# Making all modulation columns of a hybrid layer on TensorE: one change to the opening of a kernel

## The chip, the cores and the metric

The kernel runs on one core of a Trainium2 chip. A core has five engines that run side by side, each through its own list of instructions in order: TensorE (PE in the profile; it multiplies and transposes into the PSUM banks), VectorE (DVE), ScalarE (ACT), GpSimd (POOL) and SyncE (SP, which here issues the loads and stores). They wait for one another through semaphores. The metric is the device time of one execution in microseconds (us), the median over runs.

## The reference

One layer over 1024 latent tokens and 256 context tokens of width 1024, batch 1, in float32:

```python
sh1, sc1, g1, sh2, sc2, g2 = split(silu(c) @ w_ada + b_ada, 6)
csh1, csc1, *_             = split(silu(c_ctx) @ w_ada + b_ada, 6)
hx = rmsnorm(x, norm1_g) * (1 + sc1) + sh1
hc = rmsnorm(ctx, norm1_g) * (1 + csc1) + csh1
# hx @ w_in, hc @ w_in feed neighbourhood attention (with the context keys),
# two-way retention and two gates
x = x + g1 * merge(attention, retention)
x = x + g2 * conv_ffn(rmsnorm(x, norm2_g) * (1 + sc2) + sh2)
out = rmsnorm(x, final_norm_g)
```

The case is about the first two lines: shift and scale of the first modulation, for the latent tokens (from c) and for the context (from c_ctx). That is 2 x 1024 values for each of the two vectors, each a sum over 1024 products.

## The kernel before

**Layout.** Channels lie in the partitions after a transpose: a block kb of 128 channels (kb = 0 to 7) is a tile of 128 partitions by tokens. Tokens come in two halves of 512 (half 0 and 1) and one context block of 256. A shift or scale column is one number per partition for a block; `acol` holds them by vector s (0 for c, 1 for c_ctx), block kb and kind i (0 shift, 1 scale).

**The opening** (about the first 90 us of the profile) makes the modulated input and the first projection. Its pieces, with the lines under which the profile shows them:

- `load_x(tb)` loads a block of 128 tokens (8 latent ones, 8 and 9 are context). `square_x` (L162, ScalarE) sums squares, `rstd_x` (L166, L167, GpSimd) makes the inverse root, `scale_x` (L170, VectorE) scales the block in place.
- `transp(tb, (kb,), tag)` (L197, TensorE) transposes one 128 x 128 piece into a PSUM tile of its channel block. PSUM tiles come from three rings: "c0" and "c1" with three banks each, later the sums of the first projection, and "tp" with two banks, through which everything else goes. `evac_t` (L205) copies such a tile to SBUF (tile low) to free its bank.
- `mod_h` (L217, ScalarE) writes scale*x + shift rounded to the high part (tile hx, or hc for the context), `mod_v` (L221, VectorE) the same in full (tile vh or vc), `mod_l` (L226, VectorE) the difference, the low part. `ctx_h`, `ctx_v`, `ctx_l` are these three for a context block of channels.
- `load_first(half)` loads three weight blocks of the first projection (q, k and v of a head pair), `split_hi` (L319, ScalarE) and `split_lo` (L322, VectorE) split them into high and low parts. `first_mm(half, kb)` (L121 to L123, TensorE) does nine matmuls of 512 columns: three products of high and low parts for q, k and v. It needs both parts of the block's modulated input; for kb of 4 and more it needs the weights of load_first(1).
- `load_bc(i)` loads one of the vectors c and c_ctx broadcast over partitions (tile cs), `silu_bc(i)` (L245, ScalarE) takes its SiLU. `decays(h)` (L553 to L558) makes six exponentials of one column for a retention head; they are the first to need another function table, whose load the profile shows as ACT_TABLE_LOAD.
- `next_load`, `next_hi` (L589), `next_lo` (L592) bring the first weights of the second head pair; `next_mm` and `ctx_mm` (L110 to L112) are the projections behind the opening. In between, `ev_hi` and `ev_lo` (L401 to L419) move the sums of the first projection out of PSUM: q, k and v of the first head pair. next_mm writes into two banks that the ring "tp" has used.

**Two ways to a column.** The constant NPE = 2 divides the blocks.

- Blocks 0 to 3 come in two groups of two blocks, on TensorE: `load_ag(g, q)` loads a quarter of the group's weights (512 KB), `ag_mm(g, q)` (L259) multiplies SiLU of both vectors (two columns) with it, 512 wide, in two matmuls of float32, each two instructions in the profile. After four quarters `ag_ev` (L263) copies the resulting two rows to SBUF, `ag_tr` (L268) turns them into columns in four small transposes, `ag_fin` (L274, L275, VectorE) adds the bias and multiplies the scales with the norm's gain.
- Blocks 4 to 7 come as sums over a row: `load_ada(kb)` loads shift and scale weights of a block, transposed (two tiles of 512 KB). Each of the 16 sums is either one multiply-and-sum on VectorE (`ada_stt`, L297) or a product on GpSimd (`ada_prod`, L303) and a sum on ScalarE (`ada_sum`, L307); eight of each. `ada_fin` (L292, L293) adds bias and gain.

**Order.** The opening stands in `with tc.manual_schedule()`: each engine executes its pieces in the order of the text. What follows (attention by head pairs, retention by heads, the merge, the conv-FFN) is ordered by a planner, apart from a few groups. Rings of buffers set when loads can start: 14 tiles of 512 KB hold the token blocks and the modulation weights, three tiles of 256 KB the raw projection weights.

Of the kernel before, what the change touches and what calls it, by code (L numbers as in the profile page):

```python
# [11 lines left out]
ALU = mybir.AluOpType  # L12
# [21 lines left out]
NPE = 2  # L34
# [6 lines left out]
def tile_hybrid_layer(ctx, tc: tile.TileContext, io, dbg=None):  # L41
# [190 lines left out]
    cs2 = [(s0 if i else csp).tile([P, D], F32, name=f"cs{i}") for i in range(2)]  # L232
    wad = {}
# [7 lines left out]
    def load_bc(i):  # L241
        sync.dma_start(cs2[i], io["cvec"][i : i + 1].to_broadcast([P, D]))

    def silu_bc(i):
        act.activation(cs2[i], cs2[i], AF.Silu)  # L245
# [34 lines left out]
    def load_ada(kb):  # L280
        wad[kb] = [s_tile("x", 14) for _ in range(2)]
        for i in range(2):
            sync.dma_start(wad[kb][i], io["w_ada1"][kb - 2 * NPE, i])


    acol = cpool.tile([P, 2, KB, 2], F32, name="acol")

    def ada_fin(kb, s, eng):
        t = acol[:, s, kb]
        eng = pool if eng == "pool" else vec  # L290
        bb = cst["b"][:, 0:16].rearrange("p (i k) -> p i k", i=2)
        eng.tensor_tensor(t, t, bb[:, :, kb], ALU.add)  # L292
        eng.tensor_tensor(t[:, 1:2], t[:, 1:2], cst["g"][:, 0, kb : kb + 1], ALU.mult)  # L293
        (ca if s else cx)[kb] = (t[:, 1:2], t[:, 0:1])

    def ada_stt(kb, s, i):
        vec.scalar_tensor_tensor(s_tile("aj", 1), wad[kb][i], 1.0, cs2[s], ALU.mult, ALU.mult, accum_out=acol[:, s, kb, i : i + 1])  # L297

    prods = {}

    def ada_prod(kb, s, i):
        prods[kb, s, i] = s_tile("prod", 3)
        pool.tensor_tensor(prods[kb, s, i], wad[kb][i], cs2[s], ALU.mult)  # L303
# [232 lines left out]
    def ada_col2(i):  # L536
        w = ada2[i]
        late(vec.scalar_tensor_tensor(w, w, 1.0, cs2[0], ALU.mult, ALU.mult, accum_out=col[:, 16 + i : 17 + i]))  # L538
        if i + 1 < 32:
            ada_load()  # L540
# [71 lines left out]
    with tc.manual_schedule():  # L612
# [124 lines left out]
        load_bc(0)  # L737
        silu_bc(0)
        load_first(1)
        load_ada(4)  # L740
        ada_prod(4, 0, 1)
# [16 lines left out]
        load_ada(6)  # L758
# [8 lines left out]
        split_lo(1, 2)  # L767
        mod_v(True, 1, 2)
# [32 lines left out]
        ada_stt(5, 0, 0)
        square_x(9)
        ada_prod(6, 0, 0)
        ada_sum(6, 0, 0)
        mod_v(True, 1, 4)
        ada_prod(6, 0, 1)
        ada_sum(6, 0, 1)
        ada_stt(5, 0, 1)
        square_x(8)
        mod_l(True, 1, 4)  # L810
        ada_fin(6, 0, "pool")
        mod_v(True, 0, 6)
        mod_h(True, 1, 6)
        transp(4, (5,), ("tp",))
        transp(5, (5,), ("tp",))
        first_mm(0, 4)
# [3 lines left out]
        ada_fin(5, 0, "pool")  # L820
        mod_h(True, 1, 5)
        mod_v(True, 1, 6)
        mod_h(True, 0, 5)
        first_mm(1, 4)
        rstd_x(8, 2)
        scale_x(9)
        mod_h(True, 0, 6)
        silu_bc(1)
        scale_x(8)
        transp(8, (2,), ("tp",))  # L830
        transp(9, (2,), ("tp",))
        ctx_h(2)
        mod_l(True, 1, 6)
        first_mm(1, 6)
        transp(8, (0,), ("tp",))
        mod_v(True, 1, 5)
        mod_l(True, 1, 5)
        decays(1)
        ctx_v(2)
        ctx_l(2)  # L840
        mod_l(True, 0, 6)
        transp(8, (6,), ("tp",))
        transp(9, (0,), ("tp",))
        transp(9, (6,), ("tp",))
        ctx_h(0)
        evac_t(False, 0, 6, "act")
        next_load(0)
        load_ada(7)
        ada_prod(7, 0, 1)
        ada_sum(7, 0, 1)  # L850
        ada_stt(7, 0, 0)
        first_mm(0, 6)
        ctx_v(0)
        ada_prod(4, 1, 0)
        ada_sum(4, 1, 0)
        transp(8, (5,), ("tp",))
        mod_v(True, 0, 5)
        ctx_l(0)
        mod_l(True, 0, 5)
        ada_prod(7, 1, 0)  # L860
        transp(8, (1,), ("tp",))
        transp(9, (1,), ("tp",))
        ctx_v(1)
        ctx_h(1)
        transp(9, (5,), ("tp",))
        evac_t(False, 0, 5, "act")
        first_mm(1, 5)
        ada_stt(6, 1, 1)
        decays(3)
        transp(8, (3,), ("tp",))  # L870
        transp(9, (3,), ("tp",))
        transp(8, (4,), ("tp",))
        ctx_h(3)
        ada_prod(5, 1, 0)
        ada_fin(7, 0, "vec")
        ada_stt(7, 1, 1)
        ctx_v(3)
        mod_v(True, 1, 7)
        mod_v(True, 0, 7)
        ctx_l(1)  # L880
        mod_h(True, 0, 7)
        transp(9, (4,), ("tp",))
        mod_h(True, 1, 7)
        mod_l(True, 1, 7)
# [1186 lines left out]
```

## Time and profile before

| | before |
|---|---|
| median of 3 runs | 1781.46 us (1779.99 to 1782.4) |
| the profiled execution | 1783.34 us |
| its span, first to last instruction | 1781.6 us |
| mean granted TensorE clock | 0.988 |
| busy share of the span: PE, DVE, ACT, POOL | 97%, 73%, 48%, 32% |
| moved by DMA | 261.62 MB, mean 147 GB/s |

In a line of the timeline stand the start, the duration, the engine, the line of the code, the operation with its output and input tiles and their sizes, and how many instructions were merged; in brackets the idle time before and who ended it. Durations of matmuls overlap, so their cost is the distance from start to start. In the views of stretches, a line has the stretch, its length, busy time of the engines, the granted clock of TensorE (1.00 is full), the DMA share and GB/s. In the view of a tile stand the least, median and greatest duration in ns, and the first and last start. Windows of time are in us from the start of the span.

### The profile page before, as it was taken

The numbers are of one execution on the slowest core, as the hardware profiler recorded it, in microseconds if no ns is written. First come the engines' busy times: TensorE is split into PE (matmuls) and PEld (weight loads), VectorE is DVE, ScalarE is ACT, GpSimd is POOL, SyncE is SP. The second block draws the span as 40 slices with busy tenths as digits, with TensorE's granted clock in tenths as the row PEclk, the third lists the DMA queues.
The fourth block names the chain that finished last, engine by engine and source line by source line (L and its number), as shares of the span: only waits on it lengthen the run. The fifth ranks groups of instructions, "written<-read, shape, count | busy, mean of one in ns | idle before, by whom it ended". The sixth has DMA issues, their size and how long they took to land.

```text
span 1781.6 us, 24740 instructions
## 1 busy us (share of the span) xinstructions
PE 1728.4 (97%) x8357; PEld 1431.6 (80%) x8357; DVE 1309.0 (73%) x2458; ACT 850.2 (48%) x1833; POOL 569.1 (32%) x477
## 2 busy tenths in 40 slices
PE   8799999999999999999999999989999999999997
PEld 3588888888888888778877888868888888788886
DVE  5878888765776766777655556879989989875755
ACT  5667666652443434443444333544444444554444
POOL 2610000002334343554412400065555555211444
PEclk9899999999999999999999999999999999999999
DMA  9133334432231212677558633642332332586754
GB/s 344 57 116 119 113 111 137 140 112 101 70 107 48 72 39 71 205 234 252 177 178 277 224 140 138 238 137 89 107 101 89 108 118 101 165 285 195 241 160 160
DMA packets 139552, 261.62 MB, mean 147 GB/s; under 512 B 15872, under 2 KB 28320, under 8 KB 139424
## 3 DMA queue, kind: packets, MB, share of 16 engines
q1 hardware_dynamic: 139424, 260.03, 43.6%
q8 instruction: 66, 1.08, 0.3%
q14 instruction: 62, 0.51, 0.1%
HBM read 187.87 MB, written 69.48 MB: 144 GB/s over the span
## 4 chain that ended last, share of the span: by engine, by line
PE 41%; issue 6%; DVE 4%; POOL 3%; DMA 2%; ACT 1%; SPq 0%; POOLq 0%; ACTq 0%; DVEq 0%
PE u L1374 28%; PE y L1374 4%; PE pr L110 2%; PE pr L111 2%; PE pr L112 2%; PE om L121 1%; PE om L122 1%; PE om L123 1%; DVE wc L87 1%; POOL x L1885 1%; DMA ur<-in_w_up 0%; DVE v L1662 0%; DMA raw<-d_orr 0%; DVE b L1350 0%; POOL pd L1922 0%
## 5 line engine op out<-in xcount | busy, mean ns | idle before, releaser
L1374 PE MATMUL u<-T,wc 128*128 128x512 f32 x960 | 227.9, 393 | 6.4 <-ACT pu L1408 5.8
L1374 PEld LDWEIGHTS u<-T,wc 128*128 128x128 f32 x960 | 180.9, 189 | 47.6 <-ACT pu L1408 9.1
L1374 PE MATMUL y<-wc,ahl 128*128 128x512 f32 x924 | 210.7, 390 | 3.3 <-DVE wc L87 1.8
L1374 PEld LDWEIGHTS y<-wc,ahl 128*128 128x128 f32 x924 | 173.4, 188 | 40.3 <-DVE wc L87 2.5
L87 DVE TENSOR_TENSOR wc<-ur,wc 128x512 fp32r<-128x512 f32 x137 | 125.3, 917 | 65.2 <-ACT wc L86 65.1
L86 ACT CAST wc<-ur 128x512 fp32r<-128x512 f32 x137 | 85.1, 622 | 129.9 <-PE y L1374 72.1
L111 PE MATMUL mm<-low,wc 128*128 128x512 f32 (+1 forms) x328 | 124.1, 378 | 0.0
L1374 PE MATMUL u<-h2a,wc 128*128 128x512 f32 x480 | 112.3, 390 | 0.7 <-DVE pu L1417 0.7
L110 PE MATMUL mm<-hx,wc 128*128 128x512 f32 x264 | 107.5, 407 | 0.3 <-DVE vc L221 0.3
L1374 PEld LDWEIGHTS u<-h2a,wc 128*128 128x128 f32 x480 | 90.1, 188 | 19.8 <-DVE pu L1417 1.2
L112 PE MATMUL mm<-hx,wc 128*128 128x512 f32 x264 | 105.2, 399 | 0.0
L86 ACT CAST wc<-s 128x512 fp32r<-128x512 f32 x80 | 49.7, 622 | 91.5 <-PE u L1374 86.9
L123 PE MATMUL mm<-wc,low 128*128 128x512 f32 (+1 forms) x240 | 91.3, 380 | 0.0
L1508 POOL TENSOR_TENSOR col<-col,bcol 128x32 f32<-128x32 f32 x1 | 0.3, 253 | 281.5 <-DVE aw L538 281.5
L1374 PE MATMUL u<-hxT,wc 128*128 128x512 f32 x384 | 89.6, 389 | 0.0
L87 DVE TENSOR_TENSOR wc<-s,wc 128x512 fp32r<-128x512 f32 x80 | 86.4, 1082 | 2.4 <-ACT wc L86 2.0
L1374 PEld LDWEIGHTS u<-hxT,wc 128*128 128x128 f32 x384 | 72.1, 188 | 14.9
L87 DVE TENSOR_TENSOR wc<-raw,wc 128x512 fp32r<-128x512 f32 x92 | 69.5, 763 | 18.2 <-ACT wc L86 18.1
L1383 POOL TENSOR_TENSOR s<-ur 128x512 f32<-128x512 f32 x20 | 36.7, 1835 | 125.1 <-DVE wc L87 71.7
L121 PE MATMUL mm<-wc,hx 128*128 128x512 f32 x192 | 75.3, 392 | 0.6 <-ACT r L1105 0.6
L122 PE MATMUL mm<-wc,hx 128*128 128x512 f32 x192 | 75.3, 392 | 0.0
L86 ACT CAST wc<-raw 128x512 fp32r<-128x512 f32 x92 | 56.7, 621 | 32.0 <-DMA raw<-in_w_pret 5.3
(393 smaller groups left out, 4722.7 us busy)
## 6 DMA issues: line engine op xcount, KB each, us to landing
ur<-in_w_up SPq DMA_DIRECT2D x80, 256.0 KB, 3.0
ur<-d_a SPq DMA_DIRECT2D x77, 256.0 KB, 3.1
aw<-in_w_ada SPq DMA_DIRECT2D x32, 512.0 KB, 3.2
pj<-in_w_down SPq DMA_DIRECT2D x44, 256.0 KB, 4.8
d_w<-pj SPq DMA_DIRECT2D x44, 256.0 KB, 2.0
d_a<-sa SPq DMA_DIRECT2D x44, 256.0 KB, 2.0
ur<-d_w SPq DMA_DIRECT2D x44, 256.0 KB, 3.7
d_a<-at SPq DMA_DIRECT2D x33, 256.0 KB, 2.7
```

What stands on the lines that cost most here:

```text
L86: act.copy(hi, src)
L87: (lo_eng or vec).tensor_tensor(lo, src, hi.bitcast(F32), ALU.subtract)
L110: pe.matmul(out, wh, xh, start=k == 0, stop=False)
L111: pe.matmul(out, wh, xl, start=False, stop=False)
L112: pe.matmul(out, wl, xh, start=False, stop=k == n - 1)
L121: pe.matmul(out, ah, bh, start=first, stop=False)
L122: pe.matmul(out, ah, bl, start=False, stop=False)
L123: pe.matmul(out, al, bh, start=False, stop=last)
L1374: pe.matmul(out, a, b, start=first and n == 0, stop=last and n == 2, skip_group_check=True)
L1383: pool.tensor_tensor(self.s1, self.a21, self.a22, ALU.add)
L1508: pool.tensor_tensor(col[:, 16:48], col[:, 16:48], bcol[:, 16:48], ALU.add)
L1885: pool.tensor_tensor(z, z, fg[:, gs(dh)], ALU.mult)
```

## The change

NPE becomes 4, so all eight blocks go through load_ag, ag_mm, ag_ev, ag_tr and ag_fin in four groups. load_ada, ada_stt, ada_prod, ada_sum and ada_fin are gone, and so is one of the two broadcast vectors; the other is still loaded, later, since a later stage uses it. The weights of all groups are laid out on the host as those of groups 0 and 1 were.

```diff
-NPE = 2
+NPE = KB // 2
...
-    cs2 = [(s0 if i else csp).tile([P, D], F32, name=f"cs{i}") for i in range(2)]
-    wad = {}
+    cs2 = csp.tile([P, D], F32, name="cs")
...
-    def load_bc(i):
-        sync.dma_start(cs2[i], io["cvec"][i : i + 1].to_broadcast([P, D]))
+    def load_bc():
+        sync.dma_start(cs2, io["cvec"][0:1].to_broadcast([P, D]))
...
-    def load_ada(kb):
...
-    def ada_fin(kb, s, eng):
...
-    def ada_stt(kb, s, i):
-        vec.scalar_tensor_tensor(s_tile("aj", 1), wad[kb][i], 1.0, cs2[s], ALU.mult, ALU.mult, accum_out=acol[:, s, kb, i : i + 1])
...
-    def ada_prod(kb, s, i):
-        prods[kb, s, i] = s_tile("prod", 3)
-        pool.tensor_tensor(prods[kb, s, i], wad[kb][i], cs2[s], ALU.mult)
...
-    def ada_sum(kb, s, i):
-        t = prods[kb, s, i]
-        act.activation(t, t, AF.Copy, accum_out=acol[:, s, kb, i : i + 1])
...
-    w1 = w_ada[:, :2048].reshape(4, 2, P, 2, KB // 2, 2 * P)
-    out["w_ada1g"] = ac(w1[:, :, :, :, :NPE].transpose(4, 0, 2, 1, 3, 5).reshape(NPE, 4, P, 1024))
+    w1 = w_ada[:, :2048].reshape(4, 2, P, 2, NPE, 2 * P)
+    out["w_ada1g"] = ac(w1.transpose(4, 0, 2, 1, 3, 5).reshape(NPE, 4, P, 1024))
-    out["w_ada1"] = ac(w_ada[:, :2048].T.reshape(2, KB, P, D).transpose(1, 0, 2, 3)[2 * NPE :])
```

The order of the opening stays up to `first_mm(0, 3)`. From there the new text reads as follows, several calls to a line. T stands for the latent grid (True), and transp(4-7, 5) for the four calls of token blocks 4 to 7 with channel block 5; mod(half, kb) stands for mod_h, mod_v and mod_l of that block in this order, ctx(kb) for ctx_h, ctx_v and ctx_l.

```
load_first(1)  load_ag(2,0) load_ag(2,1)  transp(6,4) transp(6,7)  split_hi(1,2)  scale_x(7)
transp(7,4) transp(6,2) transp(6,0) transp(7,2) transp(7,0) transp(6,1) transp(7,1)
mod_v(T,1,1)  evac_t(T,1,4,act)  mod_h(T,1,0)  transp(7,7)  evac_t(T,1,7,act)
load_ag(2,2) load_ag(2,3)  mod_v(T,1,0) mod_l(T,1,0)  mod_h(T,1,1)  evac_t(T,1,2,act)  mod_h(T,1,2)
transp(4-6,6)  split_lo(1,2)  mod_l(T,1,1)  mod_v(T,1,2)
first_mm(0,2)  transp(4-7,3)  evac_t(T,1,3,act)  transp(7,6)  evac_t(T,1,6,act)
load_ag(3,0) load_ag(3,1)  split_hi(1,1)
first_mm(1,0)  mod_l(T,1,2)  ag_mm(2,0) ag_mm(2,1)  load_ag(3,2) load_ag(3,3)  mod_v(T,1,3) mod_h(T,1,3)
first_mm(1,1)  ag_mm(2,2) ag_mm(2,3)  ag_ev(2,act)  mod_l(T,1,3)  split_lo(1,1)  load_x(9) load_x(8)
first_mm(1,2)  ag_tr(2)  ag_fin(2)  split_hi(1,0)  mod(0,4)  split_lo(1,0)  transp(4-7,5)
first_mm(1,3)  mod(1,4)  load_bc()  load_ex()
first_mm(0,4)  ag_mm(3,0) ag_mm(3,1)  mod(0,5)  next_load(0)
first_mm(1,4)  ag_mm(3,2) ag_mm(3,3)  ag_ev(3,act)  mod(1,5)  square_x(9) square_x(8)  rstd_x(8,2)
first_mm(0,5)  ag_tr(3)  ag_fin(3)  mod(0,6)
first_mm(1,5)  mod(1,6)  scale_x(9) scale_x(8)
first_mm(0,6)  transp(8-9,2) transp(8-9,0)  mod(0,7)  ctx(2)
first_mm(1,6)  transp(8-9,1)  mod(1,7)  ctx(0)  next_hi(0)  transp(8-9,3)
first_mm(0,7)  ctx(1) ctx(3)  transp(8-9,4) transp(8-9,5)  ctx(4)  next_lo(0)  silu_bc()  decays(1)  ctx(5)
first_mm(1,7)  transp(8-9,6) transp(8-9,7)  decays(3)  ctx(6) ctx(7)  decays(0) decays(2)  dec_scale()  next_load(1)
```

Before, the same stretch went as follows (the modulations of halves and blocks in single steps, mixed with the sums):

```
first_mm(0,3)  load_bc(0) silu_bc(0)  load_first(1)  load_ada(4)  ada_prod(4,0,1) ... scale_x(7) ... load_ada(6) ...
first_mm(0,2) ... ada_sum(4,0,1) ... load_x(9)  load_bc(1)  load_ada(5)  ada_stt(4,0,0)
first_mm(1,0) first_mm(1,1)  ada_fin(4,0)  first_mm(1,2) ... load_ex()  load_x(8) ... ada_stt(5,0,0)  square_x(9)
ada_prod(6,0,0) ada_sum(6,0,0) ... ada_prod(6,0,1) ada_sum(6,0,1)  ada_stt(5,0,1)  square_x(8)  ada_fin(6,0) ...
first_mm(0,4) first_mm(1,3)  ada_fin(5,0) ... first_mm(1,4)  rstd_x(8,2)  scale_x(9)  silu_bc(1)  scale_x(8) ...
first_mm(1,6) ... decays(1) ... next_load(0)  load_ada(7)  ada_prod(7,0,1) ada_sum(7,0,1)  ada_stt(7,0,0)
first_mm(0,6) ... ada_prod(4,1,0) ada_sum(4,1,0) ... ada_prod(7,1,0) ...
first_mm(1,5)  ada_stt(6,1,1)  decays(3) ... ada_prod(5,1,0)  ada_fin(7,0)  ada_stt(7,1,1) ...
first_mm(0,5) first_mm(1,7)  ada_prod(6,1,0) ada_sum(7,1,0) ada_fin(7,1) ada_sum(5,1,0) ... ada_stt(4,1,1) ... next_hi(0) next_lo(0)
decays(0) ... ada_fin(4,1) ... ada_stt(5,1,1) ... ada_sum(6,1,0) ... decays(2)  ada_fin(5,1) ... ctx_l(6)  dec_scale()
first_mm(0,7)  next_load(1)
```

More of the change, by code (lines that the diff above doesn't have):

```diff
@@ L819, in tile_hybrid_layer @@
         first_mm(1, 3)
-        ada_fin(5, 0, "pool")
-        mod_h(True, 1, 5)
+        mod_h(True, 1, 4)
+        mod_v(True, 1, 4)
+        mod_l(True, 1, 4)
+        load_bc()
+        load_ex()
+        first_mm(0, 4)
+        ag_mm(3, 0)
+        ag_mm(3, 1)
+        mod_h(True, 0, 5)
+        mod_v(True, 0, 5)
+        mod_l(True, 0, 5)
+        next_load(0)
+        first_mm(1, 4)
+        ag_mm(3, 2)
+        ag_mm(3, 3)
+        ag_ev(3, "act")
+        mod_h(True, 1, 5)
+        mod_v(True, 1, 5)
@@ L843, in tile_hybrid_layer @@
[L843 to L860, printed above, removed]
+        first_mm(1, 6)
         transp(8, (1,), ("tp",))
@@ L895, in tile_hybrid_layer @@
[L895 to L916 removed]
+        first_mm(0, 7)
+        ctx_h(1)
@@ new lines, in tile_hybrid_layer @@
+        ctx_v(1)
+        ctx_l(1)
+        ctx_h(3)
+        ctx_v(3)
+        ctx_l(3)
+        transp(8, (4,), ("tp",))
+        transp(9, (4,), ("tp",))
+        transp(8, (5,), ("tp",))
+        transp(9, (5,), ("tp",))
+        ctx_h(4)
+        ctx_v(4)
+        ctx_l(4)
+        next_lo(0)
+        silu_bc()
+        decays(1)
+        ctx_h(5)
+        ctx_v(5)
+        ctx_l(5)
+        first_mm(1, 7)
+        transp(8, (6,), ("tp",))
+        transp(9, (6,), ("tp",))
+        transp(8, (7,), ("tp",))
@@ L917, in tile_hybrid_layer @@
+        transp(9, (7,), ("tp",))
+        decays(3)
+        ctx_h(6)
+        ctx_v(6)
+        ctx_l(6)
+        ctx_h(7)
+        ctx_v(7)
+        ctx_l(7)
+        decays(0)
+        decays(2)
         dec_scale()
-        first_mm(0, 7)
         next_load(1)
```

157 lines of the change are left out of this document (51 added, 106 removed).

## The prediction

> **What bounds the kernel now.** First the page's busy line, then the stretches behind the opening, then the waits of PE between 28 and 125 us, then the timeline of each engine in the opening.
>
> ```profile
> PE 1728.4 (97%) x8357; PEld 1431.6 (80%) x8357; DVE 1309.0 (73%) x2458; ACT 850.2 (48%) x1833; POOL 569.1 (32%) x477
> ```
>
> ```profile
> 740.00:1000.00 260.00, 252.44 (x1085) 205.10 (x1084) 170.01 (x210) 106.15 (x179) 100.81 (x68) 0.98 0.66 220
> 1000.00:1781.60 781.60, 762.83 (x3367) 626.73 (x3365) 602.88 (x785) 346.94 (x570) 297.35 (x200) 0.99 0.45 154
> sum 1671.60, PE 1640.71 PEld 1372.48 DVE 1229.63 ACT 783.89 POOL 527.57; mean PE 410.18 PEld 343.12 DVE 307.41 ACT 195.97 POOL 131.89
> ```
>
> In each stretch stand its length and PE's busy time first; the sum is over all stretches from 110 us to the end. There PE is idle for 1671.6 − 1640.7 = 30.9 us, 7.6 and 18.8 of them in the last two stretches: a PE-bound kernel, so what the opening gains or loses at its end is what the whole gains or loses. The change lies in the opening, and there PE waits:
>
> ```profile
> PE c L122 <- DVE low L226: 5.7, 2, 3.7
> PE tp L197 <- DVE vc L221: 4.5, 1, 4.5
> PE tp L197 <- DVE x L170: 4.5, 2, 2.8
> ```
>
> These are 14.7 us, all of them on VectorE (total, times, longest). VectorE is late partly because of its own column sums and partly because GpSimd slows it:
>
> ```profile
> 16.32 0.75 DVE L170 TENSOR_SCALAR x<-x,rstd 128x1024 f32<-128x1024 f32 x1 [1.96 <-POOL rstd L167]
> ...
> 35.60 3.53 DVE L170 TENSOR_SCALAR x<-x,rstd 128x1024 f32<-128x1024 f32 x2
> ```
>
> Alone the scaling of a block takes 0.75 us; two of them beside the first product on GpSimd (line L303 below, from 35.9) take 3.53 instead of about 1.45. Long waits then cost PE a second time, through its clock:
>
> ```profile
> 53.66 0.49 PE L122 MATMUL c<-low,wc 128*128 128x512 f32 x1 [3.68 <-DVE low L226]
> ...
> 55.15 0.59 PE L122 MATMUL c<-low,wc 128*128 128x512 f32 x1
> ...
> 58.79 0.39 PE L121 MATMUL c<-hx,wc 128*128 128x512 f32 x1
> ```
>
> Behind the wait of 3.68 us the matmuls of 512 columns go from about 0.23 us start to start to about 0.42, from 55.15 to 58.5: a slow stretch of 3.4 us, which costs 1.6.
>
> **What goes.**
>
> ```profile
> L303 POOL TENSOR_TENSOR prod<-x,cs x8: 2404/2791/3315, 35.9 to 76.4; 128x1024 f32<-128x1024 f32 x8
> L297 DVE SCALAR_TENSOR_TENSOR aj<-x,cs x8: 1214/1218/2535, 43.4 to 88.7; 128x1024 f32<-128x1024 f32 x8
> ```
>
> Eight sums of 1.22 on VectorE (9.8 us), eight products of 2.79 on GpSimd (22.3 us) and with them the slowing of VectorE, eight sums on ScalarE, one of two SiLUs of a broadcast vector, and GpSimd's small finishing steps.
>
> ```profile
> 29.28 1.80 SPq L283 DMA_DIRECT2D x<-in_w_ada  x4
> ```
>
> ```profile
> 30.00:50.00 20.00, 18.32 (x96) 14.64 (x94) 17.20 (x22) 14.40 (x24) 8.29 (x7) 1.00 0.87 315
> ...
> 80.00:90.00 10.00, 8.43 (x29) 6.62 (x29) 7.82 (x16) 7.91 (x21) 4.02 (x7) 0.71 0.26 89
> ```
>
> Bytes stay: sixteen quarters of 512 KB instead of eight and eight rows of 512 KB, and one broadcast load fewer. The new loads take the places of the old ones in SP's queue, from 29.3 us on, right behind the first weights of the second half. Their first use is at 43 us below. Nothing in SP's queue waits there longer than before: each quarter takes a buffer whose last reader has run by 29, the two context blocks, the broadcast vector and the decay constants come behind the quarters, and the next weights (next_load) behind those, all wanted after 65. The queue holds 5 MB, which at the 315 GB/s of the stretch from 30 to 50 is 16 us, so the last ones land near 46, and the second group is wanted from 60 on. I cost the loads at nothing, hidden under 14 us; without that cover each would cost its own 1.7 us (512 KB at that rate).
>
> **What comes.**
>
> ```profile
> 20.44 0.41 PE L268 MATMUL tp<-ident,arow 2*128 2x2 f32 x4
> 20.78 0.33 PE L197 MATMUL c<-ident,x 128*128 128x128 f32 x1
> 21.11 3.59 PE L259 MATMUL tp<-x,ccol 128*2 128x512 f32 x8
> 24.64 0.44 PE L197 MATMUL c<-ident,x 128*128 128x128 f32 x2
> ```
>
> Two quarters take 24.64 − 21.11 = 3.53 us of PE, so a group of four 7.06, two groups 14.1; each group's four small transposes 0.35 (20.44 to 20.78), 0.7 in all. ScalarE gets two copies of a row, VectorE two pairs of small finishing steps (taken as 0.4 a pair, below the 0.75 of any full operation above; the wait for them counts in the walk).
>
> ```profile
> 19.41 0.58 ACT L263 COPY arow<-tp 2x512 f32<-2x512 f32 x1 [4.04 <-PE tp L259]
> ```
>
> **PE's sum.** Up to the projection step first_mm(0, 3), which ends at 37.14, both orders are the same. From there before:
>
> ```profile
> 37.14 0.38 PE L197 MATMUL tp<-ident,x 128*128 128x128 f32 x2
> 39.18 0.33 PE L197 MATMUL tp<-ident,x 128*128 128x128 f32 x1 [1.66 <-DVE x L170]
> 39.35 0.82 PE L197 MATMUL c<-ident,x 128*128 128x128 f32 x6
> 40.00 0.73 PE L197 MATMUL tp<-ident,x 128*128 128x128 f32 x4
> 40.49 0.48 PE L121 MATMUL c<-hx,wc 128*128 128x512 f32 x1
> ...
> 43.11 0.48 PE L121 MATMUL c<-hx,wc 128*128 128x512 f32 x1
> ...
> 49.36 0.38 PE L197 MATMUL tp<-ident,x 128*128 128x128 f32 x2
> ```
>
> Three first_mm stand between the last two rows: 2.08 each. Thirteen are left, 27.0 us. The 38 transposes left cost 0.11 each (six from 39.35 to 40.00), 4.2. Before, the last first_mm ends at 90.2 (the row at 90.52 below, less its idle time), 53.1 us later: 31.2 of work, the rest waits and half clock. After: 31.2 + 14.1 + 0.7 = 46.0, so the end could be 83.1 if nothing waited.
>
> I now walk the new order, each engine in its own order with the durations above. scale_x(7) is done at 37.0 (39.13 before, 35.60 + 3.53), since GpSimd is silent; first_mm(0, 2) starts at 38.6 instead of 40.49. Then PE hardly waits: quarters of group 2 from 43.35 and 48.95, the row copied by 53.1 under first_mm(1, 2), its columns ready at 55.3 under transposes; first_mm(1, 3) covers the modulation of block 4 (ScalarE to 56.2, VectorE to 57.6), and first_mm(0, 4) starts at 57.65, 0.2 late. Group 3's quarters begin at 59.7 and 65.3; columns at 71.7; first_mm(0, 6) at 73.4. The context's transposes wait 0.8 for scale_x(8) (its square on ScalarE comes only behind the row copy at 69) and 1.1 for a free bank of the ring of two. So first_mm(1, 7) ends at 85.3: PE is 4.9 us ahead of before.
>
> **The tail takes most of it back.** All four decays, the table load and the SiLU now stand on ScalarE behind ctx_h(4), in the way of ctx_h(5) to (7), and with a ring of two banks PE's last transposes need ctx_h(5).
>
> ```profile
> 59.59 1.05 ACT L245 ACTIVATE cs<-cs 128x1024 f32<-128x1024 f32 x1
> ...
> 65.53 1.28 ACT L553 ACT_TABLE_LOAD   x1
> 66.83 0.29 ACT L553 ACTIVATE dec<-ex,lg 128x1 f32<-128x1 f32 x1
> ...
> 75.81 0.30 ACT L553 ACTIVATE dec<-ex,lg 128x1 f32<-128x1 f32 x1
> ...
> 76.93 0.56 ACT L217 ACTIVATE hc<-tp,acol 128x256 fp32r<-128x256 f32 x1
> ```
>
> SiLU 0.95 to the next start, table 1.30, six small ones 1.12 (75.81 to 76.93), ctx_h 0.47. ctx_h(4) starts at 83.0, so ctx_h(5) at 86.8; the transposes of block 7 at 87.4 (PE waits 2.1); decays(3), ctx_h(6) at 88.4; next_mm(1, 0) needs that bank and starts at 89.0 (PE waits 1.4). ScalarE is free at 91.6, behind decays(0) and (2). Before, at the same places:
>
> ```profile
> 90.52 0.47 PE L110 MATMUL mm<-hx,wc 128*128 128x512 f32 x1 [0.33 <-DVE vc L221]
> ...
> 102.10 0.36 PE L110 MATMUL mm<-hc,wc 128*128 128x256 f32 x1 [0.42 <-DVE qS L415]
> ```
>
> ```profile
> 91.79 0.60 ACT L86 CAST wc<-raw 128x512 fp32r<-128x512 f32 x1
> ```
>
> ```profile
> 93.08 0.68 DVE L87 TENSOR_TENSOR wc<-raw,wc 128x512 fp32r<-128x512 f32 x1
> 93.68 0.67 DVE L417 TENSOR_TENSOR kL<-c,kH 64x512 fp32r<-64x512 f32 x1
> ...
> 100.56 1.39 DVE L415 SCALAR_TENSOR_TENSOR qS<-mm,qS 64x512 fp32r<-64x512 f32 x2
> ```
>
> ScalarE goes over to evacuating at 91.8 before and 91.6 after: no gain there. VectorE begins its half at 93.68 and runs without a gap to 101.95, and ctx_mm(1) waits for that; after, it can begin behind ScalarE's first cast, at 92.2, and be done at 100.5. PE needs 11.0 us for its 48 matmuls at 0.23 a start, so it is done at 100.0 at full clock. If the two waits of 2.1 and 1.4, with only 0.2 of transposes between, bring a slow stretch as at 55.15, it costs up to 1.7: 101.7. ctx_mm(1) thus starts between 100.5 and 101.7 instead of 102.10. I take 101.2, a gain of 0.9, as half idle was enough to slow the clock at 55.15. The bounds: 1.6 gained; nothing gained if ScalarE's cast (L86) stays where it is.
>
> Two pages of the Trainium skill bear on this tail. "TensorE: Matmul & The Clock Gate", under "What's actually happening", says that the clock halves after at least one idle window of about 3.4 us. By that rule neither wait slows PE and the gain is 1.6; the trace differs, as the slow stretch at 55.15 began 1.5 us after PE was back. "ScalarE: Activation LUTs", under "What ACT_TABLE_LOAD costs", gives some 1.4 us of drain behind a table load. By it the tail is 1.4 longer and the gain about 0; the trace differs, the first exponential following 1.30 after the load began.
>
> The sum: 1781.6 − 0.9 = 1780.7 for the span. The profiled execution took 1783.34, the median of the runs is 1781.46, so the forecast as a median is 1780.6. A measurement of this kernel tells about 0.2%, 3.6 us: this is no change that shows.
>
> **Rivals.** *The clock in the context stretch: slower.* Between 75.7 and 85.3 PE waits 0.8 and 1.1, and transposes of 0.11 stand among four first_mm. If that is thin enough for two slow stretches in a row, as before between 80 and 90 (granted clock 0.71, so 58% of the time at half), first_mm(1, 6), (0, 7) and (1, 7) cost 2.1 more each, 6.2; about 0.9 is absorbed by waits. ScalarE's tail has no slack, so it all arrives: +5.3 − 0.9 = +4.4, 1785.9. It decides from two such stretches on; one (1.6) leaves the forecast standing. The same lack of slack passes on any other slip of PE. Against it: PE is never idle for over 1.1 us there, while the 1.66 ahead of 39.18 brought no slow stretch: from 43.11 on the starts are at full pace.
>
> *The planner lays the rest out otherwise: faster.* Only the opening is ordered by hand; what follows is ordered by a planner that sees another opening. Of PE's 30.9 idle us behind 110 a fifth could go: −6, 1775.5. For it: 26.4 of these lie behind 740. Against: the stages there are fed by their own loads, and a new order can as well lose.
>
> *It does nothing at all* (the gain of 4.9 is entirely eaten by ScalarE's tail): 1781.5, inside the forecast's class.
>
> **Chances.** Forecast with its bounds, 0.41: within 0.2%. The first rival and other slips without slack, 0.35: slower by over 0.2%. The second, 0.24: faster by over 0.2%. The range reaches to the two rivals and a little beyond, 1774.5 to 1788; its own range for the forecast alone is 1779 to 1783.
>
> **What would show it.** Right: no L303 in the opening, L170 at 0.75 throughout, PE without a wait over 1.2 us from 38.6 to 85, the last first_mm ending near 85.3, then two waits of PE for hc of L217, with ScalarE full from 83 to 91.6, and ctx_mm(1) at about 101. Wrong: half clock between 60 and 85; PE waiting for in_w_ada1g; the last first_mm at 88 or later; or an opening as walked and another idle sum of PE behind 110.

## The result: no change that shows

After takes 1783.95 us (median of 20 runs, 1780.82 to 1787.88), before 1782.72 on the same chip (20 runs, 1779.99 to 1786.13). The ratio is 1.0004, 95% interval [0.9997, 1.0011]: the same, as forecast. The forecast had a gain of 0.9 us in it; there is none.

The busy line of after, and the sum over the stretches from 110 us to the end (its length, then PE's busy time; PEld is TensorE's loading of weights):

```profile
PE 1738.8 (98%) x8397; PEld 1429.1 (80%) x8397; DVE 1282.2 (72%) x2444; ACT 841.7 (47%) x1816; POOL 538.8 (30%) x455
```

```profile
sum 1672.70, PE 1642.02 PEld 1371.97 DVE 1226.88 ACT 784.92 POOL 525.99; mean PE 547.34 PEld 457.32 DVE 408.96 ACT 261.64 POOL 175.33
```

PE is busy 10.4 us more, and still idle for 30.7 us behind 110 (30.9 before). The whole change lies ahead of that. There the middle of the opening did what was meant. First before, then after (length, busy time of PE, PEld, DVE, ACT, POOL, granted clock, DMA share, GB/s):

```profile
50.00:60.00 10.00, 6.34 (x22) 5.05 (x23) 9.14 (x13) 6.10 (x11) 5.64 (x8) 0.83 0.20 53
60.00:70.00 10.00, 5.18 (x18) 3.72 (x17) 9.93 (x9) 3.71 (x9) 6.57 (x3) 0.77 0.00 0
```

```profile
50.00:60.00 10.00, 10.00 (x43) 6.06 (x42) 4.48 (x9) 3.33 (x5) 0.00 (x0) 1.00 0.11 28
60.00:70.00 10.00, 10.00 (x31) 3.91 (x30) 0.11 (x1) 1.39 (x3) 0.00 (x0) 1.00 0.01 2
80.00:90.00 10.00, 5.68 (x28) 4.34 (x28) 5.79 (x14) 7.72 (x24) 0.00 (x0) 1.00 0.34 115
90.00:100.00 10.00, 9.57 (x35) 7.78 (x36) 8.11 (x13) 8.56 (x22) 4.89 (x5) 0.83 0.33 109
```

From 50 to 70 PE never waits and its clock is full, while VectorE is busy for 4.6 of the 20 us. From 80 to 90 PE stands idle for 4.3 us, and the clock is slowed in the next ten. The waits of PE in after from 28 to 125 us (total, times, longest; one of 0.4 behind ctx_mm(1) left out) and PE's own rows there:

```profile
PE tp L197 <- DVE vc L221: 3.5, 2, 2.6
PE mm L110 <- DVE vc L221: 2.0, 1, 2.0
PE tp L197 <- DVE x L170: 0.7, 2, 0.6
```

```profile
84.93 0.38 PE L197 MATMUL tp<-ident,x 128*128 128x128 f32 x2
87.95 0.44 PE L197 MATMUL tp<-ident,x 128*128 128x128 f32 x2 [2.64 <-DVE vc L221]
90.43 0.79 PE L110 MATMUL mm<-hx,wc 128*128 128x512 f32 x1 [2.04 <-DVE vc L221]
91.02 0.63 PE L111 MATMUL mm<-low,wc 128*128 128x512 f32 x1
91.45 0.63 PE L112 MATMUL mm<-hx,wc 128*128 128x512 f32 x1
...
103.22 0.35 PE L110 MATMUL mm<-hc,wc 128*128 128x256 f32 x1
```

The first projection is done at 84.9 instead of 90.2. Then come two waits, 4.7 us together, for VectorE, which reads a context bank behind ScalarE, and a stretch at half clock (starts 0.43 apart instead of 0.23). ctx_mm(1) comes at 103.22, 1.1 later than before, and the span is 1.1 longer.

**The two profiles do not start alike.** Up to first_mm(0, 3) the order is the same, yet first_mm(0, 0) begins 1.4 apart. Before, then after, from the timeline of PE:

```profile
10.20 3.02 PE L259 MATMUL tp<-x,ccol 128*2 128x512 f32 x4 [2.43 <-DMA x<-in_w_ada1g]
...
29.21 0.50 PE L121 MATMUL c<-hx,wc 128*128 128x512 f32 x1
```

```profile
10.38 1.88 PE L258 MATMUL tp<-x,ccol 128*2 128x512 f32 x4 [2.26 <-DMA x<-in_w_ada1g]
...
27.85 0.50 PE L121 MATMUL c<-hx,wc 128*128 128x512 f32 x1
```

The same four instructions ran slowed in the one profiled execution (granted clock 0.50 from 10.80 to 14.21) and at full clock in the other. So below, a point of the opening is given as its distance from the start of first_mm(0, 0). To ctx_mm(1) that is 72.9 before and 75.4 after: in these two profiles the changed part is 2.5 us slower, and an earlier start makes up for 1.4 of it. That the earlier start is chance is not shown: before and its four variants below all start between 29.2 and 29.7, after and its variants between 26.7 and 29.7, and there is one profile of each. The medians, which average over many starts, differ by 1.2, with an interval from -0.5 to 2.0.

### The profile page after: what moved, and what is told of

It reads as the page before. It is cut to its first block, busy times and chain, and to the rows that moved or that the text cites. A ratio compares the mean times of both kernels' runs of the same rounds, so it can differ in the third digit from the quotient of the medians.

```text
span 1782.7 us, 24753 instructions
## 1 busy us (share of the span) xinstructions
PE 1738.8 (98%) x8397; PEld 1429.1 (80%) x8397; DVE 1282.2 (72%) x2444; ACT 841.7 (47%) x1816; POOL 538.8 (30%) x455
## 4 chain that ended last, share of the span: by engine, by line
PE 41%; issue 6%; DVE 4%; POOL 3%; DMA 3%; ACT 1%; SPq 0%; POOLq 0%; ACTq 0%; DVEq 0%
PE u L1329 29%; PE y L1329 4%; PE pr L112 1%; PE pr L110 1%; PE pr L111 1%; PE om L123 1%; PE om L122 1%; PE om L121 1%; POOL x L1840 1%; DVE wc L87 1%; DMA raw<-d_orr 0%; DVE b L1305 0%; POOL pd L1877 0%; DVE hxT L87 0%; DMA vo<-d_h 0%
## 5 line engine op out<-in xcount | busy, mean ns | idle before, releaser
L87 DVE TENSOR_TENSOR wc<-ur,wc 128x512 fp32r<-128x512 f32 x137 | 122.8, 898 | 65.6 <-ACT wc L86 65.6
L86 ACT CAST wc<-ur 128x512 fp32r<-128x512 f32 x137 | 85.1, 622 | 130.6 <-PE y L1329 72.5
L1329 PE MATMUL u<-hxT,wc 128*128 128x512 f32 x384 | 89.6, 389 | 0.0
L87 DVE TENSOR_TENSOR wc<-s,wc 128x512 fp32r<-128x512 f32 x80 | 84.9, 1064 | 3.2 <-ACT wc L86 2.8
L121 PE MATMUL mm<-wc,hx 128*128 128x512 f32 x192 | 75.2, 392 | 0.6 <-ACT r L1060 0.6
L122 PE MATMUL mm<-wc,hx 128*128 128x512 f32 x192 | 75.2, 392 | 0.0
```

Of the source, the lines that this page charges most:

```text
L86: act.copy(hi, src)
L87: (lo_eng or vec).tensor_tensor(lo, src, hi.bitcast(F32), ALU.subtract)
L121: pe.matmul(out, ah, bh, start=first, stop=False)
L122: pe.matmul(out, ah, bl, start=False, stop=False)
L1329: pe.matmul(out, a, b, start=first and n == 0, stop=last and n == 2, skip_group_check=True)
```

## The experiments

All twelve in one table: start of first_mm(0, 0) and of ctx_mm(1) in the profile, their distance, the median, and the ratio to before with its interval (three kernels have a single run, the profiled one). The medians of before, taken again beside each group of kernels, lie between 1782.4 and 1784.0.

| | first_mm | ctx_mm(1) | distance | median us | ratio to before |
|---|---|---|---|---|---|
| before | 29.21 | 102.10 | 72.9 | | |
| after | 27.85 | 103.22 | 75.4 | 1783.95 | 1.0004 [0.9997, 1.0011] |
| e1_tail | 26.90 | 101.01 | 74.1 | 1782.35 | 0.9990 [0.9978, 1.0002] |
| e2_half | 29.71 | 102.07 | 72.4 | 1783.55 | one run |
| e3_fill_mm | 27.66 | 102.72 | 75.1 | 1781.6 | one run |
| e5_order | 27.98 | 97.15 | 69.2 | 1778.76 | 0.9972 [0.9959, 0.9986] |
| e6_quarter | 26.70 | 91.50 | 64.8 | 1774.89 | 0.9949 [0.9934, 0.9964] |
| e7_no_sums | 29.48 | 81.96 | 52.5 | 1762.02 | 0.9885 [0.9871, 0.9898] |
| e8_no_pool | 29.70 | 84.62 | 54.9 | 1763.29 | one run |
| e9_order2 | 29.09 | 95.86 | 66.8 | 1774.14 | 0.9954 [0.9940, 0.9968] |
| e10_pool_back | 29.35 | 106.55 | 77.2 | 1788.1 | 1.0025 [1.0014, 1.0035] |
| e11_all_vec | 29.50 | 93.57 | 64.1 | 1774.01 | 0.9945 [0.9924, 0.9966] |
| e12_unread | 29.60 | 99.07 | 69.5 | 1780.07 | 0.9989 [0.9976, 1.0002] |
| e13_mixed | 27.32 | 93.21 | 65.9 | 1774.61 | 0.9961 [0.9949, 0.9972] |

From ctx_mm(1) to the end of the span it is 1679.5 us before and after, and 1676 to 1682 in every other profile: what the opening gains or loses arrives, to within some 3 us. A distance comes from one profile; one slow stretch more or less moves it by 1.4 to 2 us, so that differences below 2 between single rows say little.

### The tail: e1, e2, e3

e1 takes the SiLU and all decays out of ScalarE's tail:

```diff
         load_ag(2, 3)
+        load_ex()  load_bc()
...
         mod_h(True, 1, 3)
+        silu_bc()  decays(1) decays(3) decays(0) decays(2)
...
-        load_bc()  load_ex()
...
-        silu_bc()  decays(1)
...
-        decays(3)
...
-        decays(0) decays(2)
```

> The kernel after with one edit: SiLU of the broadcast vector and all four decays (with the table load) moved from the end of ScalarE's opening to its idle stretch behind mod_h(1, 3), where it waits from 42.7 to 51.9 us; their loads go behind load_ag(2, 3). Theory (ScalarE's tail gave the gain back): the last first_mm still ends near 85.1, the transposes of block 7 follow at about 85.6 instead of 87.95, next_mm starts at about 87.5 instead of 90.43 and at full clock, ctx_mm(1) at 98.6 instead of 103.22, and the median falls by about 4.6 us against the kernel after, to 1779 to 1780. Rival (the ring of two banks and its two readers in a row are the limit, not ScalarE's queue): next_mm moves by less than 1 us, and the time stays. Rival (the 14 us of products on PE are the price): the same, no change.

```profile
85.79 0.44 PE L197 MATMUL tp<-ident,x 128*128 128x128 f32 x2 [0.24 <-DVE vc L221]
88.09 0.50 PE L110 MATMUL mm<-hx,wc 128*128 128x512 f32 x1 [1.86 <-DVE vc L221]
...
101.01 0.36 PE L110 MATMUL mm<-hc,wc 128*128 128x256 f32 x1
```

In e1's rows of PE the wait of 2.64 has shrunk to 0.24. The other stays, 1.86 instead of 2.04, and so does a slow stretch (89.6 to 93.0). From the transposes of context block 3 (80.06 in after, 80.30 in e1) to next_mm it is 10.4 in after and 7.8 in e1: ScalarE's extra work in the tail costs PE 2.6, not the 4.6 expected. And e1 loses 1.2 ahead of that, waiting for scale_x (1.9 in all against 0.7). A partial miss: the median was to fall by 4.6 and cannot be told from before's.

e2 is e1 with decays(0) and decays(2) left at the end.

> As e1_tail, but decays(0) and decays(2) stay at the end, behind ctx_h(7), where nothing of PE's waits for them. Theory: PE is released by ctx_h and ctx_v alone, so next_mm starts as in e1_tail (87.5) and ctx_mm(1) at 98.6, although ScalarE begins to move out the sums 2.2 us later. Rival (ScalarE's evacuation behind the opening is the bound): ctx_mm(1) is some 2 us later than in e1_tail.

From block 3's transposes (81.54) to next_mm (89.33) it is again 7.8, and from there to ctx_mm(1) 12.7 against 12.9 in e1: these two decays cost PE nothing where they stood. The early loss of e1 is gone as well: the wait for scale_x is 0.5, and as a distance block 3's transposes come at 51.8, against 53.4 in e1. Why e1 loses there was not followed further.

e3 leaves the tail and fills PE's first wait with ten matmuls whose result nobody uses.

```diff
         first_mm(1, 7)
+        fill_pe(6, 10, "mm")
         transp(8, (6,), ("tp",))
```

> The kernel after, with ten matmuls of 512 columns more in front of the transposes of context block 6, into the same bank, which the transposes then overwrite: they lie in PE's wait from 85.3 to 87.95 and keep it busy. Theory (half idle of a few us is enough for a slow stretch): next_mm still starts at 90.4, but its first matmuls follow at 0.23 instead of 0.43, and ctx_mm(1) starts 1.4 us earlier, near 101.8. Rival (the wait of 2.0 just ahead of next_mm is what slows the clock): next_mm is as slow as before and ctx_mm(1) stays at 103.2.

```profile
84.33 2.43 PE L203 MATMUL tp<-hx,wc 128*128 128x512 f32 x10
86.61 0.38 PE L197 MATMUL tp<-ident,x 128*128 128x128 f32 x2
87.36 0.44 PE L197 MATMUL tp<-ident,x 128*128 128x128 f32 x2 [0.38 <-DVE vc L229]
89.84 0.50 PE L110 MATMUL mm<-hx,wc 128*128 128x512 f32 x1 [2.04 <-DVE vc L229]
```

The rival was right: the slow stretch still comes, from 90.64 to 94.0, and from next_mm to ctx_mm(1) it is 12.9 as in after (12.8). With the first wait filled but for 0.4, the wait of 2.04 is enough to bring it on.

### The order: e5 and e9

e5 brings the context in early, each of its blocks between two projection steps, and the SiLU and decays with it; from first_mm(1, 0) on (X is transp(8-9, kb)):

```
load_x(9) load_x(8) load_ex() load_bc() load_ag(3, 0-3) next_load(0) ... first_mm(1,0) ... ag_mm(2,0) ag_mm(2,1) ...
square_x(9) square_x(8) rstd_x(8,2) silu_bc() decays(1) ... scale_x(9) scale_x(8)
first_mm(1,1) X(0) ag_mm(2,2) ag_mm(2,3) ctx(0) decays(3) ag_ev(2)   first_mm(1,2) X(1) ag_tr(2) ag_fin(2) mod(0,4) ctx(1) ...
first_mm(1,3) X(2) mod(1,4) ctx(2)   first_mm(0,4) mod(0,5) mod(1,5) X(3) ag_mm(3,0) ag_mm(3,1) ctx(3) next_hi(0) next_lo(0)
first_mm(1,4) X(4) ag_mm(3,2) ag_mm(3,3) ctx(4) decays(0) ag_ev(3)   first_mm(0,5) X(5) ag_tr(3) ag_fin(3) mod(0,6) ctx(5)
first_mm(1,5) X(6) mod(1,6) mod(0,7)   first_mm(0,6) X(7) ctx(6) mod(1,7)
first_mm(1,6) ctx(7)   first_mm(0,7) first_mm(1,7)  decays(2)
```

> The kernel after with the opening reordered behind first_mm(0, 2), no instruction added or taken away: the context blocks are loaded ahead of group 3's quarters, squared and scaled while ScalarE and VectorE wait for group 2 (43 to 52 us), their transposes go one pair at a time between the steps from first_mm(1, 1) on, SiLU and decays into ScalarE's idle time, and the opening ends with first_mm(0, 7) and (1, 7) without transposes behind them. Theory: PE's work from 37 us is 46 us, so the last first_mm ends at about 83.5, next_mm follows at once at full clock, ctx_mm(1) starts at about 94.6 (103.2 in after, 102.1 in before), and the median falls by 8 to 9 us against after, to 1775 to 1776. Rival (VectorE's and ScalarE's evacuation of the first projection takes over): ctx_mm(1) not before 97, a gain of 5 to 6. Rival (what follows absorbs it): the gain at ctx_mm(1) is there, and less than half of it at the end.

```profile
62.79 3.60 PE L258 MATMUL tp<-x,ccol 128*2 128x512 f32 x8 [1.88 <-DVE vh L221]
```

6.2 us less than after, not all that was expected: group 3's products wait 1.88 for a bank that VectorE had yet to read. The start of ctx_mm(1), 97.15, is the first rival's, but its cause is not: from next_mm to ctx_mm(1) it is 11.1, and PE doesn't wait there. No slow stretch follows this wait, though it is as long as e1's (more in the last section). e9 puts ag_mm(3, 0) and ag_mm(3, 1) ahead of X(3).

> The order of e5_order with one more exchange: the products of group 3 come ahead of the transposes of context block 3, so that they take the bank that context block 2 frees and do not wait for the modulation of block 5 (1.9 us in e5_order). Theory: that wait goes, the last first_mm ends 1.9 earlier, ctx_mm(1) starts at 95.3 instead of 97.15, and the median is 7 us below the kernel before. Rival (the wait moves to the next user of the bank): ctx_mm(1) stays at 97.

The whole list of PE's waits from 28 to 125 in e9, and ctx_mm(1):

```profile
PE tp L197 <- DVE acol L273: 0.3, 1, 0.3
```

```profile
95.86 0.36 PE L110 MATMUL mm<-hc,wc 128*128 128x256 f32 x1
```

Same products, same pieces, no waits: the distance is 66.8, 8.6 less than after and 6.1 less than before, and the kernel is 0.46% faster than before.

### The price of each way: e6, e7, e8, e12

e6 is after with one quarter of the products of groups 2 and 3 instead of four.

```diff
     def ag_mm(g, q):
+        if g >= 2 and q:
+            return
```

> The kernel after with only the first of four quarters multiplied in groups 2 and 3 (loads stay): three quarters of the sums for channel blocks 4 to 7 are left out, six times 1.76 us of PE. Theory (the products lie on PE's path, as PE hardly waits from 36 to 75): the last first_mm ends some 10 us earlier (75), the tail behind it is as long as in after, ctx_mm(1) starts near 93, and the median falls by 9 to 10 us. Rival (VectorE's and ScalarE's steps behind the columns would be late next): less than half of it.

The distance falls by 10.6, which is three quarters of the 14.1 us that the prediction had for the products. The waits of the tail are as in after (2.64, then 2.04): nothing of the products' time was hidden. The agreement to a tenth is in part chance: up to next_mm the distance falls by 11.3, and behind it e6 loses 0.8 to a longer slow stretch (eleven slowed starts from next_mm on, in after seven).

e7 and e8 take the old way apart: e7 is before with neither products nor sums (constants in their place), e8 is before without GpSimd's products alone.

```diff
# e7
     def ada_stt(kb, s, i): / ada_prod / ada_sum
+        return
# e8
     def ada_prod(kb, s, i):
+        return
     def ada_sum(kb, s, i):
-        t = prods[kb, s, i]
+        t = wad[kb][i]
...
```

> The kernel before without its eight multiply-and-sums on VectorE, eight products on GpSimd and eight sums on ScalarE (a constant stands in the columns of blocks 4 to 7; loads and finishing steps stay). It shows what the old way cost in all. Theory (sums on VectorE and the port GpSimd shares with it made PE's 14.7 us of waits and the slow stretches): ctx_mm(1) starts at about 91 instead of 102.1 and the median falls by 10 to 12 us, so that the 14 us of products on PE just replace it. Rival (PE waits there for other reasons, such as the order): a gain below 5 us.

> The kernel before without GpSimd's eight products alone: ScalarE sums the raw weights instead (the factor is left out), VectorE's eight sums stay. It parts the slowing through GpSimd from VectorE's own sums. Theory: VectorE's stretched operations (two of L170 in 5.63 and 3.53, single ones of 2.83, 2.63, 2.59, 2.54) go back to below 0.8 each and 1.5 for a pair, PE's waits between 28 and 90 fall from 14.7 to about 8, and ctx_mm(1) starts at about 97. Rival (GpSimd only filled idle time of VectorE): the waits stay at 14 and ctx_mm(1) moves by less than 1.

ctx_mm(1) lies at 81.96 in e7 and 84.62 in e8. Both expectations were far too small: the old way cost 20.4 us, and all but 2.4 of it hung on eight products on GpSimd, which PE never waits for here. The two scalings of the context, before, then in e8:

```profile
58.73 5.63 DVE L170 TENSOR_SCALAR x<-x,rstd 128x1024 f32<-128x1024 f32 x2 [0.86 <-POOL rstd L167]
```

```profile
53.96 1.42 DVE L170 TENSOR_SCALAR x<-x,rstd 128x1024 f32<-128x1024 f32 x2 [0.86 <-POOL rstd L167]
```

That could be the products' slowing of VectorE, or the waits for products that came late. e12 keeps the products and lets nobody read them:

```diff
     def ada_sum(kb, s, i):
-        t = prods[kb, s, i]
+        t = wad[kb][i]
...
```

In e8 and e12 the output of ScalarE's sum goes to a tile that nobody reads; in e12 the products have a ring of two tiles instead of three.

> The kernel before with its eight GpSimd products kept in place and read by nobody: ScalarE sums the raw weights instead (so the products are left out of eight columns of the result's input). It takes away the wait for the products and keeps them beside VectorE. Theory 'sharing': the two scalings L170 beside the first product still take about 5.6 us, VectorE's steps are stretched as before, ctx_mm(1) at 98 or later against 102.1 before, and the time is within 5 us of before. Rival 'lateness of the products': with nobody waiting ctx_mm(1) is at 84 to 88 as without products (84.6), and the time 16 to 20 us below before.

Rows of GpSimd and of VectorE in e12:

```profile
59.05 13.46 POOL L303 TENSOR_TENSOR prod<-x,cs 128x1024 f32<-128x1024 f32 x5
```

```profile
59.13 5.64 DVE L170 TENSOR_SCALAR x<-x,rstd 128x1024 f32<-128x1024 f32 x2 [0.86 <-POOL rstd L167]
64.68 2.83 DVE L226 TENSOR_TENSOR low<-vh,hx 128x512 fp32r<-128x512 f32 x1
67.44 0.80 DVE L221 TENSOR_SCALAR vh<-tp,acol 128x512 f32<-128x512 f32 x1
68.27 2.02 DVE L226 TENSOR_TENSOR low<-vh,hx 128x512 fp32r<-128x512 f32 x1
```

The slowing it is. Of the old way's 20.4 us, 2.4 are the sums (e7 to e8), 14.6 the products' presence beside VectorE (e8 to e12), 3.4 what is left (e12 to before, where ScalarE waits for products and GpSimd for ScalarE); the first and the last, differences of single profiles, are rough. VectorE's rows alone account for the 14.6: eight of its steps, as many as there are products, are 15.4 us longer in all in e12 than the same steps in e8, and from 72.72 on (58.26 in e8) every step of VectorE comes 14.5 later, as ctx_mm(1) does. PE's clock, 0.75 from 60 to 70 in e12 and full in e8, adds nothing to that, as VectorE doesn't wait longer for PE there. Nor do VectorE's waits for GpSimd's small steps, which stand in one queue with the products, grow from e8 to e12.

### Back in the new order, and other ways out: e10, e11, e13

e10 is e9 with eight products that nobody reads.

```diff
+        junk_pool(9, 8)   # x2 before first_mm(1, 2), x2 before first_mm(0, 4), x4 before first_mm(0, 5)
```

> The order of e9 (all columns on TensorE, PE without waits up to 90) with eight products on GpSimd put beside it, of the size of before's and read by nobody, from first_mm(1, 2) to first_mm(0, 5). Theory 'sharing': VectorE steps beside a product take two to four times as long, the opening gets late by 5 to 15 us, ctx_mm(1) at 101 to 111 against 95.9, and PE waits for VectorE again. Rival 'VectorE has slack in this order': steps stretched but ctx_mm(1) within 2 us of 95.9.

Rows of GpSimd, VectorE and PE in e10:

```profile
49.05 20.28 POOL L261 TENSOR_TENSOR junk<-x 128x1024 f32<-128x1024 f32 x8 [1.53 <-DVE x L170]
```

```profile
56.71 2.21 DVE L277 TENSOR_TENSOR acol<-acol,gcol 128x4 f32<-128x4 f32 x1
58.95 2.66 DVE L221 TENSOR_SCALAR vh<-low,acol 128x512 f32<-128x512 f32 x1
...
67.03 0.53 DVE L221 TENSOR_SCALAR vc<-tp,acol 128x256 f32<-128x256 f32 x1
```

```profile
67.62 0.69 PE L197 MATMUL tp<-ident,x 128*128 128x128 f32 x2 [8.17 <-DVE vc L221]
```

Eight products, idle work, cost 10.4 us of distance, although VectorE had room in this order: 8.2 are one wait of PE for VectorE, the rest is mostly the slow stretch behind it (to 71.9).

e11 is before with all sixteen sums on VectorE and no product anywhere:

```diff
     def ada_prod(kb, s, i):
+        return
     def ada_sum(kb, s, i):
+        return ada_stt(kb, s, i)
```

> The kernel before with all sixteen sums on VectorE as single multiply-and-sum steps: no product on GpSimd, no sum on ScalarE, nothing more on TensorE, same order. Computes the whole result. Theory 'the old way cost its 20 us through GpSimd's products': VectorE gets eight more sums of 1.22, 9.8 us at most, and every VectorE step runs at its lone duration, so ctx_mm(1) lies between 85 (as with no products) and 95, and the time between 1763 and 1774, 9 to 20 us faster than before. Rival 'VectorE itself bounds the opening': the added 9.8 us come on top of before's VectorE work, ctx_mm(1) is at 98 or later and the time within 4 us of before.

Distance 64.1: eight sums more on VectorE cost 9.2 against e8 (8 x 1.22 = 9.8; on PE's side 6.0 of it are waits, and a slow stretch from 71.8 to 75.2 adds some 1.6), and it is 8.8 less than before. Two lines changed give what the best of the new orders gives: 0.55% faster than before.

e13 is e9 with the last two blocks as eight sums on VectorE, three groups left on PE.

> The order of e9 with three groups of columns on TensorE and the last two blocks (6 and 7) as eight sums of 1.22 us on VectorE, no product on GpSimd. Computes the whole result. Theory 'in e9 TensorE alone paces the opening, and VectorE has room': PE loses two pairs of quarters and four small transposes, 7.3 us, VectorE gains 9.8 us where it was idle 13.4 of the 30 us from 50 to 80; ctx_mm(1) at 88.5 against 95.86, the time 7 us below e9, near 1767, 17 below before. Rival 'VectorE takes over as the bound', since two of these sums stand ahead of the modulations that TensorE needs next: PE waits 4 us or more for VectorE from 50 to 80 (e9: 0.3 in all), a slow stretch may follow, ctx_mm(1) at 93 or later and the time within 3 us of e9.

```profile
PE tp L197 <- DVE vc L221: 2.4, 2, 2.1
PE c L122 <- DVE low L226: 1.0, 1, 1.0
PE tp L197 <- DVE vh L221: 0.8, 1, 0.8
```

The rival was right: PE waits for VectorE again (its list from 28 to 125 above), and the distance falls by 0.9 of the 7.3 that PE was spared. A slow stretch follows the wait of 2.1 (62.2 to 65.6), as that rival had it. e9, e11 and e13 are not told apart by their times.

## Why the prediction was right, and where it was not

The time came out as forecast, but the mechanism only in part, and the agreement is in part luck: a gain of 0.9 us was forecast, the medians differ by 1.2 the other way and the two profiles show a loss of 2.5 in the changed part, and each of these is below the 0.2% that a measurement tells. The 1783.95 lies in the range of 1774.5 to 1788, not in the narrower 1779 to 1783 of the forecast alone; that one counts from 1781.46 for before, which took 1782.72 here.

**PE-bound, and the opening arrives: right.** 30.7 us idle behind 110; the end follows ctx_mm(1) in all fourteen profiles.

**What goes: right.** L303 is gone and L170 keeps its lone duration (least, median, greatest of six in after):

```profile
L170 DVE TENSOR_SCALAR x<-x,rstd x6: 732/748/753, 28.6 to 75.4; 128x1024 f32<-128x1024 f32 x6
```

**What comes: right.** 14.1 us of products (e6: 10.6 for three quarters), loads hidden; no wait for in_w_ada1g behind 28. e9 lies 14.3 above e7, where the columns cost nothing, against the 14.8 predicted for products and small transposes; e7 keeps the old order and 2.0 us of waits of PE (e9: 0.3), so this is only a rough agreement.

**PE's walk to the last first_mm: 1.0 too short.** As distances, it was to end at 85.3 − 29.2 = 56.1 and ended at 84.9 − 27.85 = 57.1. The mis-sized terms are small ones: scale_x(7) let PE go 0.4 later than walked, and each of the four first_mm between quarters or behind a pair of them takes 2.27 (46.03 to 48.30), not 2.08; against that, two waits were 0.4 shorter in all.

**The tail: right that it takes it back, wrong by 2.4 in how much.** Here is ScalarE, then VectorE, in after:

```profile
82.83 0.56 ACT L217 ACTIVATE hc<-tp,acol 128x256 fp32r<-128x256 f32 x1 [1.73 <-PE tp L197]
83.30 1.05 ACT L244 ACTIVATE cs<-cs 128x1024 f32<-128x1024 f32 x1
84.35 1.28 ACT L526 ACT_TABLE_LOAD   x1
85.65 0.29 ACT L526 ACTIVATE dec<-ex,lg 128x1 f32<-128x1 f32 x1
...
86.77 0.55 ACT L217 ACTIVATE hc<-tp,acol 128x256 fp32r<-128x256 f32 x1
...
91.45 0.61 ACT L86 CAST wc<-raw 128x512 fp32r<-128x512 f32 x1
```

```profile
87.35 0.54 DVE L221 TENSOR_SCALAR vc<-tp,acol 128x256 f32<-128x256 f32 x1 [2.32 <-ACT hc L217]
...
88.92 0.54 DVE L221 TENSOR_SCALAR vc<-tp,acol 128x256 f32<-128x256 f32 x1 [0.56 <-ACT hc L217]
...
89.84 0.54 DVE L221 TENSOR_SCALAR vc<-tp,acol 128x256 f32<-128x256 f32 x1
```

ScalarE's chain is as predicted to a tenth: 3.9 from ctx_h(4) to ctx_h(5) (82.83 to 86.77; predicted 83.0 to 86.8), the table load 1.30 long. What failed is the step from there to PE. The prediction freed a bank when ScalarE had read it. In the rows VectorE's reading of a bank (vc) begins only where ScalarE's has ended (86.77 + 0.55 = 87.32, then 87.35), and PE goes on behind that: 87.95, and the expected wait of 2.1 became 2.64. Then "next_mm(1, 0) needs that bank", block 6's, at 89.0: it started at 90.43, right behind the last of the three vc rows (89.84 + 0.54 = 90.38), which is block 7's. In distances: next_mm at 62.6 instead of 59.8, 1.0 of the 2.8 from the walk, 1.8 from these two. From next_mm to ctx_mm(1) it took 12.8, 0.6 more than the 12.2 allowed for. Together 3.4: a gain of 0.9 became a loss of 2.5.

**The slow stretch: right that it comes.** It follows waits of 1.9 to 2.1 (after, e1, e2, e3, e13) and one of 1.7 (e11), and did not follow the 1.88 of e5. The premise that half idle can be enough holds: ahead of the slow stretch at 55.15, from 51.76 on, PE was busy for 1.51 of 3.41 us.

**The rivals.** *The clock in the context stretch*: refuted; from 50 to 90 the granted clock of after is 1.00. *The planner lays the rest out otherwise*: refuted; the idle sum behind 110 is unchanged, and each engine's instructions behind the opening stand in the same order as before. *It does nothing at all, the gain eaten by ScalarE's tail*: that is what happened, and somewhat more.

**What the prediction did not see.** It took 4.9 us for what PE wins up to the last first_mm, and asked only whether the tail gives it back. It never asked what the old way cost as a whole. It showed one pair of steps that a product had slowed and did not add up the others. The whole was 20.4 (e7); the new one must cost only the 14 us of PE, as e9 shows. The new order spent 8.6 more: 5.9 in waits of PE (6.2 ahead of ctx_mm(1), against 0.3 in e9), 1.4 in slowed matmuls (seven starts from 90.43 on, 0.2 each), the rest unassigned.

## What to carry to other kernels

When work moves from one engine to another, price the whole of both ways by leaving each out, rather than the instructions alone: eight products on GpSimd cost 14.6 us here because VectorE's steps took a product's time beside them, and the busy share hides it, since a step held up counts as busy (VectorE 9.93 of 10 us from 60 to 70 before). Follow a PSUM bank to its last reader, and read a short ring as a chain of all its readers. Where two single profiles are compared to the microsecond, find the first point at which identical orders differ, and count from there.

## What the runs showed of the hardware

- **One VectorE step per GpSimd product.** Beside five products in a row (59.05 to 72.5 in e12, 2.69 each) stand five steps between SBUF tiles: two L170 and three L226, 2.0 to 2.8 long instead of 0.4 to 0.75. Steps that read a PSUM tile (67.44 and 67.03 above) keep their 0.80 and 0.53. The Trainium skill, "SBUF — State Buffer", under "Who interferes with whom", says that contention comes from one pair of ports that the two engines share, and that this pair is an exclusive lock. The trace agrees: how long a step takes goes by the product and not by its own size, as even the step over four columns (56.71 above) took 2.21 in e10, against 0.17 in e9.
- **The clock goes by windows of a grid.** In the granted clock of all fourteen profiles every change falls on a grid of 3.41 us, another one in each execution, and each half-clock stretch ahead of the last one of the program lasts one, two or three such windows. Here are two of them in after and two in e5 (length, busy time of PE, PEld, DVE, ACT, POOL, granted clock, DMA share, GB/s):

```profile
86.83:90.24 3.41, 0.44 (x2) 0.20 (x2) 2.26 (x5) 3.41 (x16) 0.00 (x0) 1.00 0.81 297
90.24:93.65 3.41, 3.22 (x8) 2.55 (x9) 2.11 (x5) 3.39 (x12) 2.58 (x4) 0.50 0.00 1
```

```profile
59.84:63.26 3.42, 1.54 (x8) 0.78 (x7) 3.25 (x7) 1.83 (x4) 0.00 (x0) 1.00 0.01 2
63.26:66.67 3.41, 3.41 (x10) 0.79 (x9) 1.69 (x4) 0.00 (x0) 0.00 (x0) 1.00 0.11 32
```

  Between 28 and 110 us a slow stretch begins thirteen times in these profiles, each time behind a window in which PE was busy for 0.13 to 0.46 of the time; behind one of 0.48 or more none begins. Near the edge both happen: e1 slows behind 0.46 (its wait of 1.86), e5 does not behind 0.45 (its wait of 1.88), and why is open. So the length of a wait does not decide alone; where it falls in the grid does too. The Trainium skill, "TensorE: Matmul & The Clock Gate", under "What's actually happening", has a free-running window of about 3.4 us. The length and the chance in it agree; that a window must be idle does not, since PE was at work in each of the thirteen.
- The start of first_mm(0, 0) in these fourteen profiles goes from 26.70 to 29.71 us with one and the same order ahead of it.
